# Giving tiles of whole 512-byte rows their places in SBUF first, alike modulo 512, in a two-layer hybrid diffusion backbone

## The chip, the core and the metric

The kernel runs on one NeuronCore of a Trainium2 chip. The metric is the device time of one execution in microseconds (us), lower is better. The core has TensorE (PE in the profile, with its weight loads shown apart as PEld), VectorE (DVE), ScalarE (ACT), GpSimd (POOL) and SyncE (SP), which issues all the transfers (DMA). Its on-chip memory SBUF has 128 partitions; a tile has the same byte address in each of them. That address modulo 512 is called the tile's *place* below.

## What is computed

Two layers over 256 latent tokens and 256 context tokens of width 1024, in float32. Each layer is a half-step SwiGLU feed-forward part, a token mixer, and another half-step SwiGLU; each of them begins with an RMSNorm and a shift, scale and gate computed from a conditioning vector.

```python
def swiglu(h, w1, w3, w2):
    return (jax.nn.silu(h @ w1) * (h @ w3)) @ w2

def half_ffn(h, g, shift, scale, gate, w1, w3, w2):
    return h + 0.5 * gate[:, None, :] * swiglu(modulate(rms_norm(h, g), shift, scale), w1, w3, w2)

for l in range(DEPTH):
    ...
    x = half_ffn(x, norm_g[l, 0], mod_x[0], mod_x[1], mod_x[2], ffn_w1[l, 0], ffn_w3[l, 0], ffn_w2[l, 0])
    ...
    if l % 2 == 0:
        y_x, y_c = mixer_ab(...)
    else:
        y_x, y_c = mixer_cd(...)
    x = x + mod_x[5][:, None, :] * y_x
    x = half_ffn(x, norm_g[l, 2], mod_x[6], mod_x[7], mod_x[8], ffn_w1[l, 1], ffn_w3[l, 1], ffn_w2[l, 1])
```

The inner width of the feed-forward part is 2816. `mixer_ab` is grouped-query attention beside multi-head latent attention, `mixer_cd` a chunkwise gated recurrence (HGRN2) beside neighbourhood attention; both have one combined input projection and one output projection.

## The kernel before

**Precision.** [...] To keep float32 accuracy each operand is split into a rounded part and a rest (names ending in H and L, or wh and wl), and `mm3` (L732) adds three products: rounded weight by rounded input and weight rest by rounded input, in turn over the rows k, and then rounded weight by input rest.

```python
        for k in range(nk):
            mm(ps, wh[:, k], x(xh, k), start=first and k == 0, stop=False)
            mm(ps, wl[:, k], x(xh, k), start=False, stop=False)
        for k in range(nk):
            mm(ps, wh[:, k], x(xl, k), start=False, stop=last and k == nk - 1)
```

So for one weight tile of a feed-forward part there are 16 matmuls that stream hH, in pairs, and 8 that stream hL; each matmul loads its own 128 by 128 weights (512 bytes in a partition, called a row of the weight tile here) and streams 512 columns (2048 bytes), 256 from the latent and 256 from the context tokens. In the last feed-forward part only latent tokens are left; there `mm2` (L743) alternates 512-wide matmuls (rounded and rest side by side) with 256-wide ones.

**Weights.** A ring of two tiles `raw` (and at times `ada`) receives each weight tile of 128 x 1024 from HBM (`_load`, L519); ACT rounds it into one of six tiles `wh`, and DVE or POOL puts the rest into one of six tiles `wl` (`_prep`, L530). The normed input stands in `hH` and `hL` (`norm_open`, L655), the gated product of the feed-forward part in `gH` and `gL` (`ffn`, L764). The attention output projection (`out_round`, L1046) is called twice (end of `ab`, L1134): first with both parts of its input in the tile of hH, then with the rounded part in the tile `m8` (m in the profile) and the rest in the two tiles `ada`; its weights are wh and wl again, and its matmuls come as 8 in pairs and 4 single ones.

**Order.** The program is recorded first: every operation goes into a list, with what it reads and writes. `schedule`, `latest` and `justified` (L271, L340, L391) then simulate the engines with a table of costs and set the order on each engine, and `issue` (L406) emits the instructions in that order. All of them stand under L411 in the profile for that reason.

**Places.** A tile's place is settled late. `Buf.make` (L64) asks the pool for a tile the first time that an emitted instruction uses it, and the pool gives each new tag the next free address, rounded to 32 bytes; later tiles of the same tag share the address. So the places follow the order of first use, and small tiles (a column of 4 or 8 bytes takes 32) push the large ones behind them off by 32 bytes at a time. A row inside a tile lies a multiple of 512 bytes from its start for all operands of the large matmuls, so that the place of the tile is the place of each of its rows.

Of the kernel before, what the change touches and what calls it, by code (L numbers as in the profile page):

```python
# [9 lines left out]
F32 = mybir.dt.float32  # L10
# [116 lines left out]
def is_bytes(dt):  # L127
    return 1 if dt == U8 else 4
# [6 lines left out]
class Program:  # L135
# [255 lines left out]
    def justified(self):  # L391
# [11 lines left out]
            o.engine, o.call, o.start = e, c, t  # L403
        return best[0], best[1]

    def issue(self, nc):  # L406
        end, order = self.justified()
        fix = lambda v: v.real() if isinstance(v, View) else v
        for o in order:
            for e, name, a, k, _ in [o.call] + o.more:  # L410
                getattr(getattr(nc, e), name)(*[fix(v) for v in a], **{n: fix(v) for n, v in k.items()})  # L411
        return end
# [7 lines left out]
        return lambda *a, **k: self.prog.record([(self.eng, name, a, k)])  # L420


D = 1024
KC = 8
S = 256
# [24 lines left out]
class Builder:  # L450
# [144 lines left out]
    def cond(self):  # L595

        self.cb = self.t("m8", [128, 2, D])
        for s in range(2):
            cr = self.t("ada", [128, 1024], bufs=2)
            self.load(cr, self.ap["cvec"][s : s + 1, :].to_broadcast([128, D]))  # L600
            self.nc.scalar.activation(self.cb[:, s, :], cr, AF.Silu)
# [85 lines left out]
    def norm_head(self, s, bank_a=6, rb=None):  # L687
# [9 lines left out]
        rs = self.t("nrs", [128, 2], bufs=2)  # L697
        self.rsqrt(sums, rs, D, [128, 2])
        q["rb"] = self.bank(7)[:, :S] if rb is None else rb
# [939 lines left out]
def pack(inp):  # L1639
# [6 lines left out]
    o["adaT"] = inp["ada_w"].transpose(0, 2, 1).reshape(144, 128, 1024)[16:]  # L1646
    a0 = inp["ada_w"][0][:, : 2 * D].reshape(8, 128, 2, 8, 128)
    o["ada0"] = a0.transpose(3, 1, 0, 2, 4).reshape(8, 128, 8, 256)
# [76 lines left out]
```

## Time and profile before

| | |
|---|---|
| median of 3 runs | 1843.43 us (1839.15 to 1844.44) |
| profiled execution, its own time | 1838.09 us |
| span of the profiled execution | 1836.3 us |
| PE busy | 1799.2 us, 98% |
| DVE, ACT, POOL busy | 1257.4, 744.7, 152.3 us |
| DMA, mean rate | 140 GB/s |
| mean granted TensorE clock | 0.996 of full |

The profile is of one execution. Busy times count an instruction from start to end; the matmuls overlap, and an end of a matmul is modelled, so the distance between the starts of two matmuls tells how fast they follow each other, and the listed duration of one doesn't. In a timeline row the first number is the start, the second the time to the end of the last instruction in the row.

### The profile page before, as it was taken

Reading aid. Unit: us, or ns where it says so; the run is one execution under the profiler, and the core shown is the slowest. Engines: PE = TensorE matmul, PEld = TensorE weight load, DVE = VectorE, ACT = ScalarE, POOL = GpSimd, SP = SyncE. Lnnn points to the kernel's source line nnn. Section 1 sums busy time; section 2 is a strip of 40 time slices with the busy share of each in tenths; the row PEclk is TensorE's granted clock in tenths of the full one; section 3 lists DMA queues with packets and bytes.
Section 4 is the critical chain, followed back from the end, with each engine's and each line's share of the span. In section 5 each row is a group of like instructions: output and inputs, shape, how many; then the busy total and the mean of one; then the engine's idle time right before and its main releaser. Section 6 shows DMA issues by size and latency. Waiting matters only on the chain.

```text
span 1836.3 us, 25848 instructions
## 1 busy us (share of the span) xinstructions
PE 1799.2 (98%) x9795; PEld 1494.0 (81%) x9795; DVE 1257.4 (68%) x2300; ACT 744.7 (41%) x1276; POOL 152.3 (8%) x482
## 2 busy tenths in 40 slices
PE   7999999999899999999999999999999999989999
PEld 4888888898686898888888988888888877888887
DVE  6577777668778676665756865445458768867775
ACT  5422222236567452122222522222225647756553
POOL 0000000003521000000000000000004202310000
PEclk9999999999999999999999999999999999989999
DMA  8455555513111144444443454445443422245663
GB/s 347 134 186 182 189 180 182 172 50 100 40 47 58 58 146 164 149 162 152 168 155 109 141 172 149 153 153 176 145 139 91 134 84 70 62 145 185 183 196 103
DMA packets 75691, 257.58 MB, mean 140 GB/s; under 512 B 9392, under 2 KB 13232, under 8 KB 74288
## 3 DMA queue, kind: packets, MB, share of 16 engines
q1 hardware_dynamic: 75568, 255.94, 42.3%
q8 instruction: 77, 1.26, 0.3%
q14 instruction: 46, 0.38, 0.1%
HBM read 254.86 MB, written 1.05 MB: 139 GB/s over the span
## 4 chain that ended last, share of the span: by engine, by line
PE 90%; DVE 4%; ACT 4%; issue 1%; POOL 1%; DMA 0%; ACTq 0%; DVEq 0%
PE b L411 90%; ACT gL L411 2%; DVE w L411 1%; DVE wl L411 1%; ACT wh L411 1%; DVE hL L411 0%; ACT w L411 0%; DVE gH L411 0%; DVE m L411 0%; DMA xX<-in_xT 0%; POOL rq_w L411 0%; ACT L411 0%; ACT gH L411 0%; DVE nacc L411 0%; ACT m L411 0%
## 5 line engine op out<-in xcount | busy, mean ns | idle before, releaser
L411 PE MATMUL b<-hH,wh 128*128 128x512 f32 (+1 forms) x1648 | 605.4, 385 | 1.8 <-DVE hH L411 1.8
L411 ACT CAST wh<-raw 128x1024 fp32r<-128x1024 f32 (+4 forms) x310 | 312.2, 1008 | 672.4 <-PE b L411 525.8
L411 PE MATMUL b<-hH,wl 128*128 128x512 f32 (+1 forms) x1616 | 564.7, 359 | 0.0
L411 DVE TENSOR_TENSOR wl<-raw,wh 128x1024 fp32r<-128x1024 f32 (+4 forms) x310 | 363.7, 1174 | 227.3 <-ACT wh L411 223.5
L411 PEld LDWEIGHTS b<-hH,wh 128*128 128x128 f32 x1648 | 307.8, 189 | 63.4 <-DVE hH L411 2.0
L411 PEld LDWEIGHTS b<-hH,wl 128*128 128x128 f32 x1616 | 304.9, 189 | 52.2 <-issue 1.1
L411 PE MATMUL b<-hL,wh 128*128 128x512 f32 (+1 forms) x1232 | 296.5, 376 | 0.1
L411 DVE SCALAR_TENSOR_TENSOR adas<-ada,m 128x1024 f32<-128x1024 f32 x224 | 273.5, 1221 | 9.0 <-DMA ada<-in_adaT 5.5
L411 PE MATMUL b<-gH,wh 128*128 128x512 f32 (+1 forms) x809 | 277.9, 366 | 0.0
L411 PE MATMUL b<-gH,wl 128*128 128x512 f32 (+1 forms) x809 | 263.9, 341 | 0.0
L411 PEld LDWEIGHTS b<-hL,wh 128*128 128x128 f32 x1232 | 219.7, 188 | 46.2 <-issue 1.2
L411 PEld LDWEIGHTS b<-gH,wh 128*128 128x128 f32 x809 | 150.5, 188 | 24.6
L411 PEld LDWEIGHTS b<-gH,wl 128*128 128x128 f32 x809 | 152.2, 188 | 21.6
L411 DVE SCALAR_TENSOR_TENSOR xX<-b,mod,xX 128x256 f32<-128x256 f32 x152 | 72.9, 482 | 109.7 <-PE b L411 107.8
L411 PE MATMUL b<-gL,wh 128*128 128x512 f32 (+1 forms) x633 | 138.0, 358 | 0.0
L411 PEld LDWEIGHTS b<-gL,wh 128*128 128x128 f32 x633 | 106.5, 188 | 19.3
L411 ACT ACTIVATE w<-b 128x512 f32<-128x512 f32 (+3 forms) x104 | 59.0, 567 | 140.3 <-PE b L411 137.9
L411 PE MATMUL b<-wh,hH 128*128 128x512 f32 (+3 forms) x288 | 106.3, 369 | 0.8 <-ACT hH L411 0.5
L411 PE MATMUL b<-wh,hL 128*128 128x512 f32 (+3 forms) x288 | 104.2, 364 | 1.0 <-DVE hL L411 1.0
L411 PE MATMUL b<-wl,hH 128*128 128x512 f32 (+3 forms) x288 | 104.8, 364 | 0.0
L411 DVE TENSOR_TENSOR w<-w,b 128x512 f32<-128x512 f32 x66 | 45.3, 687 | 77.9 <-PE b L411 77.6
L411 POOL TENSOR_TENSOR nacc<-nacc,w 128x256 f32<-128x256 f32 x5 | 7.3, 1457 | 735.4 <-ACT w L411 731.4
(213 smaller groups left out, 1899.5 us busy)
## 6 DMA issues: line engine op xcount, KB each, us to landing
raw<-in_w SPq DMA_DIRECT2D x182, 512.0 KB, 3.5
ada<-in_adaT SPq DMA_DIRECT2D x128, 512.0 KB, 4.4
raw<-in_w SPq DMA_DIRECT2D x56, 448.0 KB, 3.5
ada<-in_w SPq DMA_DIRECT2D x22, 512.0 KB, 3.5
gH<-in_ada SPq DMA_DIRECT2D x4, 1024.0 KB, 10.3
raw<-in_ab_out SPq DMA_DIRECT2D x8, 512.0 KB, 3.6
raw<-in_cd_z SPq DMA_DIRECT2D x8, 512.0 KB, 3.6
ada<-in_w SPq DMA_DIRECT2D x8, 448.0 KB, 3.3
```

The costliest lines, as they stand in the source:

```text
L411: getattr(getattr(nc, e), name)(*[fix(v) for v in a], **{n: fix(v) for n, v in k.items()})
```

## The change

A new step `lay_out` runs after the order is settled and before the first instruction is emitted. It collects the byte size of every tag that is not in PSUM, sorts the tags so that those whose size is a whole multiple of 512 come first (otherwise in the order of recording), and asks the pool for one tile under each tag. That fixes the addresses; the tiles that the instructions ask for later share them.

```diff
+    def lay_out(self):
+
+        size = {}
+        for ring in self.rings.values():
+            for b in ring:
+                if not b.psum:
+                    n = int(np.prod(b.shape[1:], dtype=int)) * is_bytes(b.dtype)
+                    size[b.pool, b.tag] = max(size.get((b.pool, b.tag), 0), n)
+        for (pool, tag), n in sorted(size.items(), key=lambda i: i[1] % LINE > 0):
+            pool.tile([128, n // 4], F32, tag=tag, name=f"{tag}_home")
+
     def issue(self, nc):
         end, order = self.justified()
+        self.lay_out()
         fix = lambda v: v.real() if isinstance(v, View) else v
...
+LINE = 512
 D = 1024
```

The list of instructions on each of the five engines, with shapes, queues and waits, is the same before and after, instruction by instruction; what differs in the built program are the addresses in SBUF. The places of the tiles, read from both built programs:

| tile (number of buffers) | place before | place after |
|---|---|---|
| wh (6) | 160, and five at 352 | 128 |
| wl (6) | 256, and five at 352 | 128 |
| hH, hL | 320, 352 | 128 |
| gH, gL | 0, 320 | 128 |
| m8, raw (2), ada (2) | 352 | 128 |
| xX, xC | 160 | 128 |
| w of 2 KB (4), adas | 480 | 128 |
| w of 1 KB (5) | 160, 256, and three at 0 | 128 |
| pt (3) | 160, 256, 352 | 128 |
| p (3) | 224, 288, 352 | 128 |
| ident, vA, vB, dqT | 224, 256, 32, 224 | 128 |
| columns and other small tiles | various | various |

The distances between large tiles change as well, for instance that from gH to gL, 42816 bytes before and 16384 after.

## Rows read from the trace of the kernel before

**Rows 1.** The page: busy us, share, instructions; and the chain that ended last.

```profile
PE 1799.2 (98%) x9795; PEld 1494.0 (81%) x9795; DVE 1257.4 (68%) x2300; ACT 744.7 (41%) x1276; POOL 152.3 (8%) x482
...
PE 90%; DVE 4%; ACT 4%; issue 1%; POOL 1%; DMA 0%; ACTq 0%; DVEq 0%
```

**Rows 2.** By stretch: length, busy us of PE, PEld, DVE, ACT, POOL; clock, DMA share, GB/s.

```profile
60.00:200.00 140.00, 140.00 (x603) 113.11 (x603) 102.75 (x149) 41.63 (x50) 0.00 (x0) 1.00 0.54 184
1519.00:1644.00 125.00, 115.47 (x1165) 100.91 (x1163) 98.69 (x167) 90.62 (x148) 35.94 (x89) 0.98 0.30 94
1660.00:1820.00 160.00, 160.00 (x914) 139.67 (x914) 118.95 (x177) 84.84 (x140) 1.47 (x1) 1.00 0.60 181
```

**Rows 3.** PE's matmuls by form: count | busy us, mean ns | idle before.

```profile
L411 PE MATMUL b<-hH,wh 128*128 128x512 f32 x1456 | 558.8, 399 | 1.8 <-DVE hH L411 1.8
L411 PE MATMUL b<-hH,wl 128*128 128x512 f32 x1072 | 425.3, 397 | 0.0
L411 PE MATMUL b<-hL,wh 128*128 128x512 f32 x1040 | 268.5, 393 | 0.0
L411 PE MATMUL b<-gH,wh 128*128 128x512 f32 x599 | 226.6, 395 | 0.0
L411 PE MATMUL b<-gH,wl 128*128 128x512 f32 x423 | 167.5, 396 | 0.0
L411 PE MATMUL b<-hH,wl 128*128 128x256 f32 x544 | 139.4, 283 | 0.0
L411 PE MATMUL b<-gL,wh 128*128 128x512 f32 x423 | 107.9, 396 | 0.0
L411 PE MATMUL b<-gH,wl 128*128 128x256 f32 x386 | 96.4, 281 | 0.0
L411 PE MATMUL b<-wh,hH 128*128 128x512 f32 x160 | 64.2, 401 | 0.0
...
L411 PE MATMUL b<-gH,wh 128*128 128x256 f32 x210 | 51.3, 282 | 0.0
```

**Rows 4.** Timeline of PE, a feed-forward part: start us, us, instructions merged.

```profile
75.83 1.98 PE L411 MATMUL b<-hL,wh 128*128 128x512 f32 x8
77.65 0.40 PE L411 MATMUL b<-hH,wh 128*128 128x512 f32 x1
...
81.38 2.00 PE L411 MATMUL b<-hL,wh 128*128 128x512 f32 x8
83.22 0.40 PE L411 MATMUL b<-hH,wh 128*128 128x512 f32 x1
```

**Rows 5.** Timeline of PE, the output projection, 512 wide.

```profile
617.49 0.40 PE L411 MATMUL b<-hH,wl 128*128 128x512 f32 x1
...
620.29 0.40 PE L411 MATMUL b<-hH,wl 128*128 128x512 f32 x1
...
626.92 0.39 PE L411 MATMUL b<-m,wh 128*128 128x512 f32 x1
...
629.64 0.39 PE L411 MATMUL b<-m,wh 128*128 128x512 f32 x1
```

**Rows 6.** Timeline of PE, 256 wide: the output projection's end, then the next feed-forward part.

```profile
634.73 0.62 PE L411 MATMUL b<-ada,wh 128*128 128x256 f32 x4
635.18 0.28 PE L411 MATMUL b<-m,wh 128*128 128x256 f32 x1
...
636.62 0.28 PE L411 MATMUL b<-m,wh 128*128 128x256 f32 x1
...
660.15 0.29 PE L411 MATMUL b<-hH,wh 128*128 128x256 f32 x1
...
662.03 1.11 PE L411 MATMUL b<-hL,wh 128*128 128x256 f32 x8
```

**Rows 7.** Timeline of PE, pairs that stream gH.

```profile
150.44 0.40 PE L411 MATMUL b<-gH,wl 128*128 128x512 f32 x1
...
151.15 0.40 PE L411 MATMUL b<-gH,wh 128*128 128x512 f32 x1
```

## The prediction, made before the changed kernel ran

> **What bounds the kernel now.** I read the page's busy shares and its chain of waits first, then the busy times by stretch, then the forms of TensorE's matmuls, and last the starts of single matmuls in the timeline. The first two say where an edit of places could count at all: PE is busy 98% of the span, and 90% of the chain that ended last is PE itself [rows 1]. The stretches say the same of the feed-forward parts: between 60 and 200 us PE is busy 140.00 of 140 us with 603 matmuls, DVE 102.75, ACT 41.63, and DMA 0.54 of its time, with the clock granted in full [rows 2]. Nothing there waits on DVE, ACT or DMA in a way that holds PE. So a change that alters no instruction, no order and no wait can only move the time if it alters how long a matmul holds PE.
>
> One number from that row is the base of everything below. All 603 matmuls of that stretch are 512 wide in float32r, each with its own weight load, and they follow each other without a gap: 140.00 / 603 = **232.2 ns from start to start** [rows 2]. The duration listed for one, about 0.40 us in the timeline, holds the tail that the next one overlaps, so I use distances between starts throughout.
>
> **Does that distance depend on places?** The trace before has the experiment in it, since its tiles lie at different places modulo 512 (the table ahead of the diff), and steps of a whole row keep a place.
>
> First, one group of a feed-forward part, with one pair of weight tiles, both at place 352 [rows 4]. The 16 matmuls that read hH (place 320) start at 77.65 us, and the run after them at 81.38: 3.73 / 16 = 233.1 ns. The next 8 read hL (place 352, so that the streamed tile and the weights agree) until 83.22: 1.84 / 8 = 230.0 ns; the run at 75.83 took 1.82 / 8 = 227.5 ns. Same width, same weights, same clock, yet 3 to 6 ns less.
>
> hH and hL differ in more than place: hH is read by pairs (with wh, then with wl), hL row after row. The output projection takes that doubt away [rows 5]. Its first half streams the attention result out of hH (320), its second half out of m8 and ada (352), in the same pattern of 8 paired matmuls and 4 single ones, with weights that lie at 352 in the rows shown. Twelve of the first half take 620.29 - 617.49 = 2.80 us, or 233.3 ns each; twelve of the second take 629.64 - 626.92 = 2.72 us, or **226.7 ns**. Only the places differ. This is the row nearest to what the change makes of every such matmul, and I take its value for a kernel in which all whole-row tiles lie alike.
>
> The 256-wide matmuls answer otherwise [rows 6]. With places that differ (hH at 320, the weights at 160 and 256), 16 of them take 662.03 - 660.15 = 1.88 us, or 117.5 ns. With places alike, 12 take 636.62 - 635.18 = 1.44 us, or 120.0 ns: alike is worse here. The quickest I find are the four at 634.73, 0.45 us in all or 113 ns, where ada at 352 meets wh at 160. In the last feed-forward part the two widths alternate, and 914 matmuls in 160.00 us give 350.1 ns a pair [rows 2]; less 232.2 that leaves 117.9. I take 118.0 before and 120.0 after.
>
> [...]
>
> **The change part by part.**
> - *Instructions, order, waits:* none is added, removed or moved, on any engine or DMA queue, so these cost nothing; no cover is needed, as there is nothing to cover.
> - *512-wide matmuls:* the forms listed sum to 1456 + 1072 + 1040 + 599 + 423 + 423 = 5013, and three of 160 (wh,hH; wl,hH; wh,hL; one row stands for them) make 5493 [rows 3]. At 232.2 - 226.7 = 5.5 ns each: **-30.2 us**.
> - *256-wide matmuls:* 544 + 386, the 210 of gH,wh, as many of gL,wh, and 192 each of hH,wh and hL,wh: 1734 [rows 3]. At +2.0 ns: **+3.5 us**.
> - *What is not realised:* three forms of 160 run between attention and projection work, where PE isn't alone on the path; in 1519 to 1644 us it is busy 115.47 of 125 us [rows 2]. Half of 480 x 5.5 ns goes: **+1.3 us**.
> - *DVE, ACT, POOL:* their operands move as well. The trace separates no place effect there that the path could feel; DVE has 37 us of slack in the 140 of [rows 2], which PE's gain of 2.4%, some 3 us, shortens but doesn't use up. Nothing is late next in the feed-forward parts.
> - *DMA:* the destinations move from 352 to 128 and other places. No row shows a load at 128. At a busy share of 0.54 a load that took a tenth more or less stays hidden. Only the start of the program, before the first weights are in, is exposed to loads, and I leave 1 us either way for it in the range.
>
> Sum: -30.2 + 3.5 + 1.3 = **-25.4 us**, 1.4%. The profiled execution took 1838.09 us, so it would take 1812.7. The runs shown have their median at 1843.43, 5.3 us above it; the four executions lie between 1838 and 1844, with 1841.3 as their mean. From that mean: **1816 us**.
>
> **Bounds.** The unknown is what places alike at 128 do, since the rows have them alike at 352 only. From below: 512-wide at 226.7, the best steady value that I found, and 256-wide at the 113 ns of [rows 6], which turns +3.5 into -8.7 us: -37.6 and 1804, with scatter and the first loads 1801. From above: only the 230.0 ns of [rows 4], so 5493 x 2.2 = 12.1 us less, 3.5 more and 0.6 not realised: -8.0 and 1833. I take the value in the middle of the list, since [rows 5] hold it in a run of many matmuls, and weights and stream agree there as they will everywhere.
>
> **Rivals.**
> 1. *Part of the gain (0.13).* Agreement helps only while a run lasts, and each new start pays again: for it speaks that the runs of [rows 4] hold 230.0, not 226.7. Against it: in the new layout no form ends the agreement, since hH, gH, gL, wh and wl agree too. Time: 1825 to 1836, 1833 worked out above.
> 2. *No change (0.08).* What differs in [rows 4, 5] goes with the tile and not with its place modulo 512, such as its distance from the weights over many kilobytes, which the change scrambles: some matmuls quicken, as many slow down. Against it: three streamed tiles (hL, m8, ada) show the lower values. Time: 1841, the mean of the four executions, within a few us. [...]
> 3. *Slower (0.05).* [...] The 256-wide rows show just this sign. If at 128 the 512-wide ones take it too, the nearest price is the slowest steps of the gH pairs, three in 151.15 - 150.44 = 0.71 us or 236.7 ns [rows 7]: 5493 x 4.5 = +24.7, with +3.5: 1869. It decides from a distance over 231.6 ns on, where the 512-wide gain no longer pays for the 3.5 us.
> That the tiles don't get the places the change says is out: in the built program every whole-row tile stands at 128.
>
> **How the numbers follow.** Forecast 0.74, and the rivals 0.13, 0.08 and 0.05. The forecast's own range is 1801 to 1825, rival 1 reaches to 1836; I give 1801 to 1833, which leaves out the no-change and slower cases and the last of rival 1. About 0.3%, 5.5 us, is what a measurement of this kernel can tell from none. Faster by more than that is the forecast and rival 1: 0.87; same 0.08; slower 0.05.
>
> **What would show it right or wrong.** In the profile of the changed kernel, 60 to 200 us should hold some 617 matmuls in place of 603 (140 / 0.2267), the hH, hL, gH and gL runs should all stand at 226 to 228 ns from start to start, and the 256-wide ones near 120; the last feed-forward part should gain least, 346.7 ns a pair against 350.1. Busy time of DVE and ACT should stay as it is. It is wrong if these runs still alternate around 233 ns, or if the time changes while they do.

## The result and the profile after

The changed kernel takes 1818.66 us (median of 4 runs, 1817.51 to 1819.39), against 1842.93 us for the kernel before (median of 4, 1839.15 to 1844.44). The ratio is 0.9871, with a 95% interval of 0.9854 to 0.9888: 24.3 us or 1.3% faster. The forecast of 1816 us and its range held. The profiled execution took 1817.92 us, its span is 1816.1 us.

The page of the changed kernel, busy times and the chain that ended last, for [rows 1]:

```profile
PE 1778.3 (98%) x9795; PEld 1498.3 (83%) x9795; DVE 1257.2 (69%) x2300; ACT 745.7 (41%) x1276; POOL 152.5 (8%) x482
...
PE 88%; DVE 4%; ACT 4%; DMA 2%; issue 1%; POOL 1%; SPq 0%; ACTq 0%; DVEq 0%
```

DVE, ACT and POOL are busy as long as before, to 1 us. Only PE's busy time fell, by 20.9 us, and PE still is the chain, apart from the 2% of DMA, which come up again below.

Busy times by stretch of the changed kernel (length, then PE, PEld, DVE, ACT, POOL, clock, DMA share, GB/s), for [rows 2]:

```profile
60.00:200.00 140.00, 139.83 (x618) 115.47 (x617) 104.59 (x152) 43.34 (x52) 0.00 (x0) 1.00 0.56 188
...
1660.00:1800.00 140.00, 140.00 (x802) 122.00 (x801) 104.61 (x156) 72.81 (x117) 0.00 (x0) 1.00 0.58 176
```

The same stretch of the last feed-forward part in the kernel before:

```profile
1660.00:1800.00 140.00, 140.00 (x800) 122.23 (x800) 104.45 (x154) 74.71 (x123) 1.47 (x1) 1.00 0.63 189
```

Between 60 and 200 us there are 618 matmuls in place of 603. In the last part there are 802 in place of 800: next to nothing was won there.

Timelines of PE in the changed kernel (start, time to the end of the last one merged, instruction). First a group of a feed-forward part, for [rows 4], then pairs that stream gH, for [rows 7], the output projection's 512-wide matmuls, for [rows 5], and 256-wide ones, for [rows 6]:

```profile
75.32 1.98 PE L423 MATMUL b<-hL,wh 128*128 128x512 f32 x8
77.13 0.39 PE L423 MATMUL b<-hH,wh 128*128 128x512 f32 x1
...
80.76 1.98 PE L423 MATMUL b<-hL,wh 128*128 128x512 f32 x8
82.57 0.39 PE L423 MATMUL b<-hH,wh 128*128 128x512 f32 x1
...
148.31 0.39 PE L423 MATMUL b<-gH,wh 128*128 128x512 f32 x1
...
151.94 0.39 PE L423 MATMUL b<-gL,wh 128*128 128x512 f32 x1
...
612.08 0.39 PE L423 MATMUL b<-hH,wl 128*128 128x512 f32 x1
...
614.80 0.39 PE L423 MATMUL b<-hH,wl 128*128 128x512 f32 x1
...
620.01 0.39 PE L423 MATMUL b<-m,wh 128*128 128x512 f32 x1
...
622.73 0.39 PE L423 MATMUL b<-m,wh 128*128 128x512 f32 x1
...
632.48 0.28 PE L423 MATMUL b<-m,wh 128*128 128x256 f32 x1
...
633.92 0.28 PE L423 MATMUL b<-m,wh 128*128 128x256 f32 x1
```

The 16 matmuls that stream hH now take 80.76 - 77.13 = 3.63 us, 226.9 ns each (233.1 before), the 8 of hL 1.81 us, 226.3 ns (230.0 before), the 16 of gH 3.63 us. In the output projection both halves take 2.72 us for twelve: the half that read hH has come down from 2.80 us to what the other half had before. Twelve 256-wide ones take 1.44 us, 120.0 ns each.

**Where the profiled spans differ from the medians.** The two profiled spans are only 1836.3 - 1816.1 = 20.2 us apart, 4 us less than the medians. The difference lies in the mixer of the first layer, where the clock is granted in part: followed from matmul to matmul, which have the same order in both kernels, the lead of the changed kernel is 7.3 us at the mixer's start (412 us in the kernel before) and 3.9 us at 490 us. In stretches of 8 us, the kernel before:

```profile
412.00:420.00 8.00, 6.53 (x48) 5.92 (x49) 7.82 (x32) 6.68 (x18) 1.47 (x2) 1.00 0.07 14
...
460.00:468.00 8.00, 3.84 (x16) 3.02 (x15) 4.69 (x8) 2.15 (x4) 6.81 (x36) 0.86 0.30 97
468.00:476.00 8.00, 7.69 (x41) 6.33 (x41) 6.94 (x13) 4.97 (x8) 3.91 (x21) 0.93 0.02 3
```

And the changed kernel, which comes to the same places some 7 us sooner:

```profile
404.00:412.00 8.00, 6.43 (x37) 5.59 (x36) 7.15 (x22) 5.84 (x15) 1.47 (x2) 0.79 0.01 2
...
452.00:460.00 8.00, 3.84 (x18) 2.89 (x17) 6.40 (x9) 2.65 (x5) 5.74 (x29) 0.94 0.48 138
460.00:468.00 8.00, 8.00 (x30) 6.72 (x31) 4.85 (x9) 4.63 (x7) 5.38 (x30) 0.64 0.03 10
```

In both, PE is idle for more than half of one such stretch (3.84 of 8 us busy), and the granted clock is low during it and behind it: 0.86 and 0.93 before, 0.94 and 0.64 after. These are means: in shorter stretches it reads 0.50 from 465.8 to 469.0 us before and 1.00 from 404 to 465, and 0.50 from 459.0 to 465.7 us after and 1.00 from 466 to 479. The first dip, 0.79 in a stretch with 1.6 us of idle PE, is not in the profile of before at all, though PE is idle for 1.5 us there. The stretches with 0.64 and 0.79 alone hold 8 x 0.36 + 8 x 0.21 = 4.6 us of clock that was not granted. It does not go with the places: the same 500 matmuls of that mixer (numbers 1900 to 2400) take 95.8 us before at a mean clock of 0.98, 99.1 after at 0.93, 97.5 with all tiles at 160 (below) at 0.95, and 100.0 at 0.93 with the weights out of step (below), where the gain is gone.

### The profile page after: what moved, and what is told of

It reads as the page before. It is cut to its first block, busy times and chain, and to the rows that moved or that the text cites. A ratio compares the mean times of both kernels' runs of the same rounds, so it can differ in the third digit from the quotient of the medians.

```text
span 1816.1 us, 25848 instructions
## 1 busy us (share of the span) xinstructions
PE 1778.3 (98%) x9795; PEld 1498.3 (83%) x9795; DVE 1257.2 (69%) x2300; ACT 745.7 (41%) x1276; POOL 152.5 (8%) x482
## 4 chain that ended last, share of the span: by engine, by line
PE 88%; DVE 4%; ACT 4%; DMA 2%; issue 1%; POOL 1%; SPq 0%; ACTq 0%; DVEq 0%
PE b L423 88%; DMA raw<-in_w 1%; ACT gL L423 1%; DVE wl L423 1%; DVE w L423 1%; ACT wh L423 1%; DMA ada<-in_adaT 1%; DVE m L423 1%; ACT w L423 0%; DVE gH L423 0%; DVE hL L423 0%; DMA xX<-in_xT 0%; ACT gH L423 0%; POOL rq_w L423 0%; DVE adas L423 0%
## 5 line engine op out<-in xcount | busy, mean ns | idle before, releaser
L423 PE MATMUL b<-hH,wh 128*128 128x512 f32 (+1 forms) x1648 | 599.1, 381 | 1.8 <-DVE hH L423 1.8
L423 PE MATMUL b<-hH,wl 128*128 128x512 f32 (+1 forms) x1616 | 558.4, 355 | 0.0
```

## The experiments

The theory is that of the prediction: a 512-wide float32r matmul (the type of wh, wl, hH, hL, gH and gL, `F32R` in the kernel) takes less time when the tile that it streams and the weights lie alike. Rivals are the absolute place, long distances between tiles, and the other tiles (loads, DVE, ACT). Every kernel runs the same instructions with the same waits as the changed one, except for the last three; only addresses differ. (In the traces the 9795 matmuls have the same order in all of them.) All ratios are against the kernel before. The line numbers move with the lines added in `lay_out`.

### All whole-row tiles up by 32 bytes

```diff
-        for (pool, tag), n in sorted(size.items(), key=lambda i: i[1] % LINE > 0):
+        rows = sorted(size.items(), key=lambda i: i[1] % LINE > 0)
+        rows[0][0][0].tile([128, 8], F32, tag="pad", name="pad_home")
+        for (pool, tag), n in rows:
             pool.tile([128, n // 4], F32, tag=tag, name=f"{tag}_home")
```

> All whole-row tiles are moved up together by 32 bytes, from place 128 to place 160; their agreement stays. If agreement between the streamed tile and the weights is what counts: about 1818 us, 617 or 618 matmuls between 60 and 200 us, 226.7 ns from start to start. If it is the absolute place that counts (128 is a multiple of 128 bytes, 160 is not): the gain goes, about 1840 us and 603 matmuls.

Measured: 1817.73 us, ratio 0.9858 [0.9842, 0.9875], and in its windows view

```profile
60.00:200.00 140.00, 140.00 (x619) 115.95 (x619) 101.92 (x148) 41.75 (x50) 0.10 (x2) 1.00 0.53 181
```

619 matmuls, against 618 after the change. That the tiles start at a multiple of 128 does not matter here.

### Only the weights moved, by 32 bytes

```diff
+        kind = lambda i: 2 if i[1] % LINE else int(i[0][1][:2] in ("wh", "wl"))
+        pad = True
+        for (pool, tag), n in sorted(size.items(), key=kind):
+            if pad and tag[:2] in ("wh", "wl"):
+                pool.tile([128, 8], F32, tag="pad", name="pad_home")
+                pad = False
             pool.tile([128, n // 4], F32, tag=tag, name=f"{tag}_home")
```

> Only wh and wl, twelve tiles, move by 32 bytes to place 160; all other whole-row tiles stay at 128. If agreement between streamed tile and weights counts: 512-wide matmuls back to about 233.3 ns, 600 to 603 matmuls between 60 and 200 us, 1840 to 1848 us (5493 x 6.6 ns = 36 us above 1818 at most, less the 3.5 us that the 256-wide ones give back). If places of the other tiles (loads, VectorE, ScalarE) make the gain: stays near 1818 us.

Measured: 1849.71 us, ratio 1.0040 [1.0027, 1.0053], slower than the kernel before:

```profile
60.00:200.00 140.00, 140.00 (x601) 112.71 (x601) 99.09 (x144) 40.85 (x49) 0.00 (x0) 1.00 0.53 180
```

601 matmuls. Twelve tiles out of step by 32 bytes take back the whole gain and 7 us more. Part of the 7 us are the runs that were alike in the kernel before (hL, m8 and ada with weights at 352, [rows 4, 5]) and are out of step here as well: between the two traces hL's 512-wide matmuls lose 3.7 us and those of m8 and ada 0.3. The rest is not shown to come from places; the profiled execution also loses 3.5 us in its first 120 matmuls, where that of the kernel with all tiles at 160, which has the whole gain, loses 4.5. The time is 1.7 us above the upper end that I had written down.

### Only TensorE's operands first, and the opposite order

```diff
-        for (pool, tag), n in sorted(size.items(), key=lambda i: i[1] % LINE > 0):
-            pool.tile([128, n // 4], F32, tag=tag, name=f"{tag}_home")
+        for (pool, tag), n in size.items():
+            if tag.rsplit("_", 1)[0] in PE_TAGS:
+                pool.tile([128, n // 4], F32, tag=tag, name=f"{tag}_home")
```

`PE_TAGS` are wh, wl, hH, hL, gH, gL, m8, ada and pt; the other tiles come in order of first use, and stand at the places of the kernel before.

> Only the tiles that TensorE streams or loads as weights in the large products (wh, wl, hH, hL, gH, gL, m8, ada, pt) get their places first and stand at 128; raw, xX, xC, w, adas, p, ident, vA, vB are back at the places that they had before the change. If the agreement of TensorE's operands is the whole cause: 1818 us within 3 us, 617 or 618 matmuls between 60 and 200 us. If transfers, VectorE or ScalarE gain by their own tiles' places: part of the gain goes, 1822 to 1840 us.

Measured: 1818.10 us, ratio 0.9870 [0.9855, 0.9885]:

```profile
60.00:200.00 140.00, 140.00 (x619) 115.91 (x619) 101.72 (x148) 41.46 (x50) 0.00 (x0) 1.00 0.54 181
```

So the places of raw, xX, xC, w, adas, p and the rest bring nothing that these runs can tell. The other kernel of this pair keeps the places and changes the distances:

```diff
-        for (pool, tag), n in sorted(size.items(), key=lambda i: i[1] % LINE > 0):
+        for (pool, tag), n in sorted(reversed(size.items()), key=lambda i: i[1] % LINE > 0):
```

> The whole-row tiles are laid out in the opposite order: all places are 128 as in the changed kernel, all distances over kilobytes differ. If places modulo 512 count: 1818 us within 3 us, 617 or 618 matmuls between 60 and 200 us. If long distances between tiles make the gain: another time, 1825 to 1841 us.

Measured: 1817.24 us, ratio 0.9859 [0.9844, 0.9874], and 619 matmuls between 60 and 200 us again:

```profile
60.00:200.00 140.00, 140.00 (x619) 115.91 (x618) 105.38 (x153) 43.13 (x52) 0.00 (x0) 1.00 0.56 188
```

Long distances do not matter here: 619 matmuls, against 618 after the change.

### How near is alike?

The weights stay at 128; the tiles that stream move. In each kernel hH, hL, m8 and ada get one distance from the weights and gH and gL another, so that two distances are read from one trace. The edit of the first of the five (the others differ in the two groups' order and in the two pads):

```diff
+        pads, names = (64, 64), (("hH", "hL", "m8", "ada"), ("gH", "gL"))
+        rank = lambda i: 3 if i[1] % LINE else next((r for r, g in enumerate(names, 1) if i[0][1].rsplit("_", 1)[0] in g), 0)
+        rows, at = sorted(size.items(), key=rank), 0
+        for i in rows:
+            while at < min(rank(i), 2):
+                rows[0][0][0].tile([128, pads[at] // 4], F32, tag=f"pad{at}", name=f"pad{at}_home")
+                at += 1
+            pool, tag = i[0]
+            pool.tile([128, i[1] // 4], F32, tag=tag, name=f"{tag}_home")
```

> Weights stay at 128; hH, hL, m8 and ada move to 192 (64 past the weights), gH and gL to 256 (128 past them). If agreement must be modulo 512: 512-wide matmuls at 233 ns for both, 1840 to 1850 us. If a smaller modulus is enough (64, 128 or 256 bytes): hH and hL, or gH and gL alone, stay at 226.7 ns.

> Weights at 128; hH, hL, m8 and ada at 384 (256 past the weights), gH and gL at 0 (384 past, or 128 short of them). Modulo 512: both at 233 ns, 1840 to 1850 us. Modulo 256: hH and hL at 226.7 ns, gH and gL at 233, some 1830 us. Modulo 128: both at 226.7, 1818 us.

> Weights at 128; gH and gL at 320 (192 past the weights), hH, hL, m8 and ada at 448 (320 past, or 192 short). The trace before had 256-wide matmuls at 113 ns where the streamed tile stood 192 past the weights: with gH so, the 256-wide ones that stream gH should take 113 ns; 512-wide ones 230 to 233 ns by agreement modulo 512, and about 1835 to 1848 us. If only a distance of some size is needed, 512-wide ones are at 226.7 ns here too.

> Weights at 128; gH and gL at 160 (32 past the weights), hH, hL, m8 and ada at 64 (448 past, or 64 short). By agreement modulo 512: 512-wide at 233 ns for both, 1840 to 1850 us. If the sign of the distance matters (a stream that runs ahead of the weights' place or behind it), the two differ by some ns from each other and from the run with the weights 32 ahead.

> Weights at 128; hH, hL, m8 and ada at 224 (96 past the weights), gH and gL at 288 (160 past). The two distances that no run has had yet. If the pattern repeats every 256 bytes and only 0 is quick: 512-wide matmuls at 230 to 233 ns for both, about 1838 to 1848 us. If 0 is not the best distance, one of the two is under 226.7 ns.

How the steps are read: one group of a feed-forward part is 24 matmuls, and the rows of hL or gL stand a group apart. The timeline of the second kernel, hH and hL 256 bytes past the weights, gH and gL 384:

```profile
109.18 1.98 PE L430 MATMUL b<-hL,wh 128*128 128x512 f32 x8
...
114.62 1.98 PE L430 MATMUL b<-hL,wh 128*128 128x512 f32 x8
...
131.20 2.03 PE L430 MATMUL b<-gL,wh 128*128 128x512 f32 x8
...
136.80 2.03 PE L430 MATMUL b<-gL,wh 128*128 128x512 f32 x8
```

5.44 us for 24 at a distance of 256 bytes is 226.7 ns, as quick as alike; 5.60 us at 384 is 233.3 ns. The first kernel, 64 and 128 bytes:

```profile
109.83 1.99 PE L430 MATMUL b<-hL,wh 128*128 128x512 f32 x8
...
115.33 1.99 PE L430 MATMUL b<-hL,wh 128*128 128x512 f32 x8
...
131.94 2.02 PE L430 MATMUL b<-gL,wh 128*128 128x512 f32 x8
...
137.52 2.02 PE L430 MATMUL b<-gL,wh 128*128 128x512 f32 x8
```

5.50 us at 64 is 229.2 ns, 5.58 at 128 is 232.5 ns. All twelve distances (stream less weights, modulo 512), as the mean from start to start of matmuls whose neighbours are of the same width and distance, taken from the same traces:

| distance, bytes | 512-wide, ns | 256-wide, ns | from |
|---|---|---|---|
| 0 | 226.9 | 119.8 | the changed kernel |
| 256 | 227.1 | 119.9 | second, hH and hL |
| 64 | 229.0 | 117.6 | first, hH and hL |
| 320 | 229.0 | 117.5 | third, hH and hL |
| 128 | 232.4 | 118.7 | first, gH and gL |
| 384 | 233.3 | 118.7 | second, gH and gL |
| 192 | 233.3 | 114.7 | third, gH and gL |
| 448 | 233.3 | 114.0 | fourth, hH and hL |
| 32 | 233.3 | 116.7 | fourth, gH and gL |
| 480 | 233.3 | 118.3 | weights moved by 32 |
| 96 | 233.3 | 119.9 | fifth, hH and hL |
| 160 | 234.2 | 117.7 | fifth, gH and gL |

The five kernels took 1832.75, 1826.47, 1833.16, 1846.26 and 1849.86 us, with ratios 0.9952 [0.9937, 0.9967], 0.9919 [0.9903, 0.9936], 0.9944 [0.9922, 0.9966], 1.0020 [1.0011, 1.0030] and 1.0034 [1.0021, 1.0047]. That is as the distances ask: matmul by matmul against the changed kernel's trace, the 512-wide ones that stream hH, hL, m8 or ada lose 6.1, 0.3, 7.5, 21.4 and 19.8 us, those that stream gH or gL 6.3, 7.4, 7.8, 7.5 and 8.6 us, of 14.1, 7.1, 15.4, 27.6 and 30.6 us in all.

What follows: over the distances measured the pattern repeats every **256 bytes**, not every 512 as the change and my theory have it (512-wide, 0 and 256, 64 and 320 agree to 0.2 ns, 192 and 448, 128 and 384 to 0.9). The expectation for a modulus of 256 was met for the second kernel; the expectation modulo 512 failed for hH and hL in the first three. The fifth kernel is 1.9 us above the upper end that I had written down, and neither of its distances is quicker than 0. Of the distances, 0 (and with it 256) is the quickest for 512-wide matmuls and among the slowest for 256-wide ones, which on the mean are quickest at 192 and 448 (64 short of the weights).

### A width by itself: the last feed-forward part in blocks

```diff
         for k in range(nk):
-            if k:
-                mm(ps[:, :S], wl[:, k], x[:, k, :S], start=False, stop=False)
-            mm(ps, wh[:, k], x[:, k, :], start=k == 0, stop=k == nk - 1)
-            if not k:
-                mm(ps[:, :S], wl[:, k], x[:, k, :S], start=False, stop=False)
+            mm(ps, wh[:, k], x[:, k, :], start=k == 0, stop=False)
+        for k in range(nk):
+            mm(ps[:, :S], wl[:, k], x[:, k, :S], start=False, stop=k == nk - 1)
```

> Places as in the changed kernel; mm2 of the last feed-forward part issues its 8 (or 7) 512-wide matmuls first and then the 256-wide ones, in place of one by one in turn. The planner reorders some matmuls ahead of that part as well. If a matmul whose neighbours have its own width takes what the runs show for it (226.9 and 119.8 ns): 346.7 ns for each of 528 pairs in place of 350.4, 2 us less, 1816 us. If agreement simply does not help where only one token half is left: 350.4 a pair still, 1818 us.

Measured: 1820.53 us (1816.73 to 1822.29), ratio 0.9870 [0.9853, 0.9886], no different from the changed kernel. Its timeline of the last part:

```profile
1701.57 2.00 PE L423 MATMUL b<-hH,wh 128*128 128x512 f32 x8
1703.41 1.11 PE L423 MATMUL b<-hH,wl 128*128 128x256 f32 x8
1704.36 2.00 PE L423 MATMUL b<-hH,wh 128*128 128x512 f32 x8
```

Eight 512-wide ones take 1.84 us, 230.0 ns each, the eight 256-wide ones 0.95 us, 118.8 ns: 348.8 ns a pair, where I had written 346.7; in turns, in the changed kernel, a pair takes 349.1. The single steps in the trace of such a run of eight are 233, 236, 229, 232, 231, 227, 227, 227 ns: after this change of width it takes five matmuls until the quick step is reached, and with eight in a run that costs some 3 ns each. In the order by turns it is never reached: the 512-wide ones of the last part take 233.7 ns on the mean in the changed kernel.

It need not be the width that changes. In the kernel before, the eight of hL that start at 81.38 us [rows 4] follow 512-wide pairs that stream hH 32 bytes short of the weights, and take 230, 236, 228, 233, 230, 227, 227 and 226 ns: the 230.0 ns of the prediction are such a start. Nor is it always five: the eight at 75.83 us take 232 ns and then 226 or 227 each.

### Each width with its own distance

Weights of products that stream 256 columns are written 64 bytes further on, in tiles that are 64 bytes longer; gaps up to the next multiple of 256 are filled with small tiles. The core of the edit, on top of the blocks:

```diff
+            while at % 256:
+                left = 256 - at % 256
+                fit = next((i for i in small if 0 < -(-i[1] // 32) * 32 % 256 <= left), None)
...
-        h = self.t("wh", [128, 1024], F32R, NW)
-        low = self.t("wl", [128, 1024], F32R, NW)
+        h, low = (self.t(t, [128, 1024 + UP], F32R, NW)[:, u * UP : u * UP + 1024] for t, u in zip(("wh", "wl"), up))
```

`UP` is 16 elements, and `up` says for each planned weight tile which of its two parts meets 256 columns.

> b1_blocks, and the weights of products that stream 256 columns stand 64 bytes further on (streamed tile 64 short of the weights, where the sweep had the 256-wide matmuls at 114.0 ns), while those of 512-wide products stay alike with the stream. If the two widths can have each its own distance: 512-wide at 226.9, 256-wide at 114 in runs of their own, 1494 x 5.9 = 8.8 us less in the mixed parts and 528 x 5.9 = 3.1 us in the last part, 1804 us. If the quick 256-wide steps depend on what runs before them: between 1805 and 1816 us.

Measured: 1814.35 us, ratio 0.9834 [0.9819, 0.9849]. That is 30 us under the kernel before in the same set of runs (1844.29 us) and a little under the changed kernel, by intervals that just do not touch; the interval of the last run below, with the same distances, does touch. The time lies in the range that I had written down for quick steps that depend on what runs before them: most of the 256-wide matmuls did not come to 114 ns. A group of 24, from its timeline:

```profile
1029.40 1.10 PE L442 MATMUL b<-hL,wh 128*128 128x256 f32 x8
1032.23 1.10 PE L442 MATMUL b<-hL,wh 128*128 128x256 f32 x8
```

In the changed kernel, and in the fourth kernel of the sweep, where the distance is the same as here:

```profile
1017.55 1.12 PE L423 MATMUL b<-hL,wh 128*128 128x256 f32 x8
1020.43 1.12 PE L423 MATMUL b<-hL,wh 128*128 128x256 f32 x8
```

```profile
1042.35 1.07 PE L430 MATMUL b<-hL,wh 128*128 128x256 f32 x8
1045.07 1.07 PE L430 MATMUL b<-hL,wh 128*128 128x256 f32 x8
```

That is 2.83, 2.88 and 2.72 us, or 117.9, 120.0 and 113.3 ns each. In the sweep the stream stood at 64 and the weights at 128 modulo 256; here it is 128 and 192. So the last run moved everything by 64:

```diff
+        home(next(iter(size))[0], "pad", 192)
         for (pool, tag), n in size.items():
             if n % LINE == 0:
                 home(pool, tag, n)
```

> b2_blocks_up with every tile 64 bytes lower modulo 256: streamed tiles and the weights of 512-wide products at 64 modulo 256, the weights of 256-wide products at 128 (they were at 128 and 192). The distances are the same, so if only the distance between stream and weights counts, nothing changes: 1814 us, 256-wide matmuls at 117.2 ns. If for the 256-wide ones the absolute places count as well (113.8 ns was measured with the stream at 64 and the weights at 128): about 2000 x 3.4 = 7 us less, 1807 us; the 512-wide ones stay at 227 ns, since agreement alone sets them.

Measured: 1813.93 us, ratio 0.9845 [0.9831, 0.9858], and 2.83 us for a group again:

```profile
1032.53 1.10 PE L443 MATMUL b<-hL,wh 128*128 128x256 f32 x8
1035.36 1.11 PE L443 MATMUL b<-hL,wh 128*128 128x256 f32 x8
```

So the absolute places modulo 256 are not it. Nor is it anything that belongs to a whole kernel, such as the step from one weight tile to the next (4096 bytes in the sweep, a multiple of 256 but not of 512 here) or the pace of the 512-wide matmuls (233 ns there, 227 here): both steps stand in one trace. In the third kernel of the sweep, where gH and gL are 64 short of the weights modulo 256:

```profile
392.00 0.28 PE L430 MATMUL b<-gH,wh 128*128 128x256 f32 x1
...
393.59 0.62 PE L430 MATMUL b<-gL,wh 128*128 128x256 f32 x4
394.04 0.60 PE L430 MATMUL b<-ident,nrs 128*128 128x128 f32 x4
394.40 0.60 PE L430 MATMUL b<-gL,wh 128*128 128x256 f32 x3
394.84 0.28 PE L430 MATMUL b<-gH,wh 128*128 128x256 f32 x1
...
396.49 0.99 PE L430 MATMUL b<-gL,wh 128*128 128x256 f32 x7
```

The 14 from 392.00 us on take 1.59 us, 113.6 ns each; four 128-wide matmuls of another product come in between; the 14 from 394.84 on, with the same streamed tile and the same distance, take 1.65 us, 117.9 ns each. From 376.8 us to the break the steps are 113 or 114 ns but for the starts, behind it 117 to 119 ns up to 402 us. The last run has the break too: 14 from 388.89 to 390.48 us take 1.59 us, 14 from 391.73 to 393.38 us 1.65 us. So at this distance there are two steps, each held until something else runs in between, and the table's 114.7 and 114.0 ns are a mixture. What decides at a break which of the two follows stays open.

## Why the prediction was right

**That places decide, and how much.** The step between the two halves of the output projection, 233.3 and 226.7 ns [rows 5], held, and so did the choice of 226.7 ns for a kernel with all tiles alike: feed-forward parts with both token halves hold 226.9 ns after the change (mean of some 4440 of their dense matmuls, 232.4 before). The experiments show the cause: moving the weights alone by 32 bytes undoes it (601 matmuls between 60 and 200 us, 603 before the change), moving all tiles together does not (619), and TensorE's operands alone carry it (619). What the prediction had wrong is the modulus: its "alike modulo 512" is more than is needed; the rows of the trace before could not tell 512 from 256, since their quick runs are at distance 0. Why TensorE takes longer at some distances no run shows.

**512-wide, -30.2 us.** Measured from start to start over all dense ones of the two traces: 232.40 ns (5503) before, 227.71 ns (5495) after, 4.7 ns and **-25.8 us**. The term was too large in two places. The 528 of the last feed-forward part got nothing (232.9 before, 233.7 after), since each stands between two 256-wide ones: 528 x (5.5 + 0.8) = 3.3 us. The forms in which wh or wl stream and hH or hL are the weights came down to 228.7 ns only, 3.7 ns less in place of 5.5: 0.9 us. For these 480 the prediction had taken off 1.3 us, though for another reason, other work beside PE.

**256-wide, +3.5 us.** Measured 118.10 ns before and 118.87 after: +1.6 us. In runs of their own they went to 119.9 ns as forecast; in the last part, by turns with 512-wide ones, they fell from 117.7 to 116.2. So the forecast of 346.7 ns a pair there failed: 140 us / 401 pairs = 349.1 ns, against 350.0 before. The step that failed is that a matmul takes the same time whatever its neighbours' width; I had carried the 226.7 of long runs over to it.

**The sum.** -25.8 + 1.6 = -24.2 us by the steps' own measures, -24.3 by the medians, -25.4 predicted. That the two are only 1.2 us apart is in part luck: the 512-wide term promised 4.4 us too much, of which the 1.3 us taken off for another reason and the 1.9 us too many that the 256-wide term charged give back 3.2.

**Hidden work at nothing.** DVE, ACT and POOL are busy as before. One new wait showed up in 60 to 200 us, PE waiting once for 0.2 us for gH. It is short, but what led to it is new. The chain of the kernel before is PE alone in this stretch:

```profile
59.98 140.24 PE b L411 x603
```

That of the changed kernel, followed back from the wait, runs from 63 to 124 us through loads, their rounding and the conditioning sums; its shares between 60 and 126 us:

```profile
by line: DMA raw<-in_w 28.8%; DMA ada<-in_adaT 22.2%; DVE wl L423 12.9%; issue 8.3%; ACT wh L423 8.0%; PE b L423 7.7%; DVE adas L423 6.2%; DVE w L423 3.2%; SPq L423 1.0%; ACT gH L423 1.0%; DVE gL L423 0.9%; DVEq L423 0.1%; ACTq L423 0.1%
```

So the loads, which the prediction called hidden, stayed so but for 0.2 us, with nothing to spare there. The kernels with all tiles at 160, with TensorE's operands alone and with the opposite order show no wait of PE between 60 and 200 us.

**Rivals.** Part of the gain (1) describes what happened in the last part: there each new start does pay again, 233.7 ns on the mean for a 512-wide one. Its argument from the 230.0 ns of [rows 4] was sound, since those are the steps of a start; in the changed kernel the parts with both token halves have no such starts, as the prediction held against it. No change (2) is excluded by the opposite order of tiles, which has the same time. Slower (3) is the sign that the 256-wide matmuls have (118.10 to 118.87 ns); the 512-wide ones have the other (232.40 to 227.71).

## What to carry to other kernels

When matmuls follow each other without a gap and each loads its own weights, look at the SBUF addresses of the streamed tile and of the weights: here their distance modulo 256 was worth 3% of a 512-wide float32r matmul, 226.9 against 233.3 ns, for no instruction at all. Which distance was quickest depended on the width (0 for 512 columns, 226.9 ns; 448 bytes for 256 columns, 114.0 ns against 119.8 at 0), so measure it for each shape in the kernel, from start to start. A trace whose tiles lie at different places already holds the comparison.

## What was not expected

- The distance counts modulo 256 in these kernels (226.9 ns at 0, 227.1 at 256), and not only as alike or not: 64 bytes past the weights costs 229.0 ns, 32 or 96 bytes 233.3.
- The slow and the quick step lie equally far apart in both widths: 233.3 - 226.7 = 6.6 ns for 512 columns, 120.0 - 113.3 = 6.7 ns for 256. They are not the only steps: the table has 229.0 ns, 256-wide ones also take 117.8, and at 64 short of the weights the 233.3 ns of the 512-wide ones are a mean of steps of 230, 231, 235 and 236 ns.
- After a change of width or of distance it can take five matmuls (233, 236, 229, 232, 231 ns) before the quick step is reached.
- The same distance, 64 bytes short of the weights, gives 256-wide matmuls a step of 113.3 or of 117.8 ns in one and the same kernel, and a short break by other matmuls can turn the one into the other.
